# Score passes of 32 rows put into four row tiles of TensorE, in a hybrid MLA and forgetting-attention block

## The chip, the core and the metric

The kernel runs on one core of one Trainium2 chip. The metric is the device time of one execution in microseconds, lower being better. Three runs of the kernel before took 632.3, 632.51 and 634.76 us; their median is 632.51 us. A profile was taken of one further execution of the same program.

## What is computed

One decoder layer over 528 positions (16 learned meta tokens ahead of 512 real ones) of width 1024. A single projection of the normalised input gives the inputs of two attention branches and of their gates. Both branches have 16 heads of width 64 and a causal softmax. The branches differ in what is added to the product of query and key:

```python
q_m = concat([q_nope, rope(q_pe, pos)])          # 64 + 32 wide
k_m = concat([k_nope, broadcast(k_pe)])          # the 32-wide rotary key is one for all heads
o_mla = causal_block_attention(q_m, k_m, v_mla, MLA_SCALE)

cum = cumsum(log_sigmoid(f_logit + fox_forget_b))
o_fox = causal_block_attention(fq, fk, fv, FOX_SCALE, cum)    # logit[t,s] += cum[t] - cum[s]

y_mla = (o_mla * silu(z_mla)) @ w_br_mla
y_fox = (o_fox * silu(z_fox)) @ w_br_fox
mixed = (sigmoid(gate_a) * y_mla + sigmoid(gate_b) * y_fox) @ w_out
out = h + rmsnorm(mixed)                          # meta tokens dropped
```

In the softmax of a row the term `cum[t]` is the same for all keys, so the kernel adds only the keys' part, `-cum[s]`.

## The kernel before

**Precision.** Float32 products are made of TensorE passes over operands that were split into a high and a low part (`wh` and `wl` of a weight, `uTh` and `uTl` of the input, entries 0 and 1 of `hlq` and `hlk` for queries and keys). A product is high by high, low by high and high by low. The weights are split as they arrive: ScalarE copies the high part (line 116) and GpSimd subtracts it for the low one (line 92). Their loads are issued on SyncE's queue (line 107) into three buffers (`wraw`).

**Stages.** The attention part goes over 8 pairs of heads, and for each pair first the forgetting branch (FoX, `br` is 1), then MLA (`br` is 0): 16 stages (line 681). A stage of TensorE is, in this order: scores of query blocks 0, 1 and 2 (`scores(0)`), the value products of the stage before (`values`, tile `ov`), scores of block 3 (`scores(1)`), and then filling work in steps: the projections for the next stage (`fq`, `fk`, `v`, `mq`, `mk`), the silu gates (`z`), the transposes of the values (`vt`, `vm`), between which the normalisations `norm(0)` and `norm(1)` are emitted (lines 725 to 737). TensorE keeps this written order (`manual_schedule`, line 415). The other engines and SyncE's queue are ordered by the framework's scheduler, which may move an instruction ahead of others that are not ready.

**Scores.** The two heads of a pair lie in partitions 0 to 63 and 64 to 127 (`hs`), so that each matmul fills 64 of the 128 rows of the array, and the two heads' matmuls are issued one behind the other. `sets` (lines 584 to 590) lists the passes over a piece of keys: the three passes of the split 64-wide product and then

- for FoX one pass with `ONE` as the stationary and `CT` as the moving operand: two rows of ones per head against two rows of `-cum/scale`, high and low part, the other 62 rows zero;
- for MLA two passes with `QP`, which holds 32 rows of the high part of the rotated query and 32 rows of its low part per head: one against `KPH`, which holds the high part of the rotary key twice, and one against `KPL`, which holds the low part of the key in the upper 32 rows of each head and zeros in the lower 32.

So FoX has 4 passes per piece and MLA has 5. Query block b sees 144 + 128 b keys. The pieces (`banks`, lines 600 and 601) are 144 and 272 columns for blocks 0 and 1, side by side in one PSUM bank per head; 400 columns for block 2 in another bank per head; and for block 3 columns 0 to 271 and 272 to 527 in two banks per head. The pool `stp` has four banks in all. VectorE reads a bank, adds the mask and finds the row's extreme (line 620, `nb`), ScalarE makes the exponentials (line 628), `norm` divides and splits the probabilities into `pn` (lines 655 and 656, the meta columns on GpSimd, lines 642 to 647), and eight DMA transposes a stage (line 661) bring them into `pt` for the value products, six for blocks 0 to 2 and two for block 3.

**Other transfers on SyncE's queue.** `CT` is loaded from `c_dram` by two transfers a pair (line 242; for pair 0 by four straight from `ch`, line 395), `QP` from `qpe_dram` by one transfer a pair (line 462). After the attention, the branch products (`py`), the gates (`pg`) and the output product (`po`) follow; the change does not touch them.

Of the kernel before, what the change touches and what calls it, by code (L numbers as in the profile page):

```python
# [11 lines left out]
F32 = mybir.dt.float32  # L12
F32R = mybir.dt.float32r
# [10 lines left out]
S = 512  # L24
# [25 lines left out]
def f32(ap):  # L50
    return ap.bitcast(F32)
# [3 lines left out]
def block_kernel(ctx: ExitStack, tc: tile.TileContext, x, meta_tokens, pre_norm_g, w_in, fox_forget_b,  # L55
                 mla_q_norm_g, mla_kv_norm_g, w_uq, w_ukv, w_br_mla, w_br_fox, w_out, post_norm_g,
                 rope_tok, rope_pe, out):
    nc = tc.nc
# [26 lines left out]
    def mm(*a, **k):  # L85
        nc.tensor.matmul(*a, **k)  # L86
# [4 lines left out]
    def split_lo(eng, lo, src, hi):  # L91
        eng.tensor_tensor(out=lo, in0=src, in1=f32(hi), op=ALU.subtract)  # L92
# [118 lines left out]
    ONE = fx.tile([128, 128], F32R, tag="ONE", name="ONE")  # L211
    nc.gpsimd.memset(f32(CT), 0.0)
    nc.gpsimd.memset(f32(ONE), 0.0)
    for h in range(2):
        nc.gpsimd.memset(f32(ONE[64 * h : 64 * h + 2, :]), 1.0)
    hls = {}

    def hl_done(key, n, w):
# [16 lines left out]
    def k_fox(pr):  # L235
        halves = hl_done(("k", 1, pr), L, HALF)

        def done(i, ps):
            halves(i, ps)
            if pr and i:  # L240
                for h in range(2):
                    nc.sync.dma_start(f32(CT[64 * h : 64 * h + 2, :]), c_dram[:, 2 * pr + h, :])
        return unit(f"fk{pr}", win_w(O_FK, pr), u_act, KD, ALLT, done)


# [2 lines left out]
    with ExitStack() as ph:  # L248
# [141 lines left out]
        nc.vector.scalar_tensor_tensor(out=ch[:, 1], in0=fa[:, 0], scalar=-1.0 / SC_FOX, in1=f32(ch[:, 0]),  # L390
                                       op0=ALU.mult, op1=ALU.subtract)

        for i in range(2):
            for h in range(2):
                nc.sync.dma_start(f32(CT[64 * h + i : 64 * h + i + 1, :]), f32(ch[h : h + 1, i]))
        for i in range(2):
            nc.sync.dma_start(c_dram[i], f32(ch[:, i]))
        run(qk[7:])
# [14 lines left out]
    with ExitStack() as att:  # L413
# [4 lines left out]
        stp = att.enter_context(tc.tile_pool(name="stp", bufs=4, space=PSUM))  # L418
        ovp = att.enter_context(tc.tile_pool(name="ovp", bufs=1, space=PSUM))

        QP = ac.tile([128, S], F32R, tag="QP", name="QP")
        KP = [ac.tile([128, L], F32R, tag=n, name=n) for n in ("KPH", "KPL")]
        maskt = ac.tile([128, L + 16], BF16, tag="maskt", name="maskt")
        nc.gpsimd.memset(maskt, 0.0)
# [12 lines left out]
            nc.gpsimd.memset(pn[b // 3][:, :, PN_STEP * b % 15, :], 0.0)  # L437
        for r in range(4):
            nc.vector.tensor_copy(KP[0][32 * r : 32 * r + 32], kpT)
        nc.gpsimd.memset(f32(KP[1]), 0.0)  # L440
        for h in range(2):
            split_lo(nc.vector, KP[1][64 * h : 64 * h + 32], kpT, KP[0][0:32])
        lctx.close()
        gpool = gctx.enter_context(tc.tile_pool(name="gpool", bufs=1, side="right"))
        gT = [gpool.tile([128, KD, S], F32, tag=n, name=n) for n in ("gT0", "gT1")]
# [3 lines left out]
        def q_mla(pr):  # L449
            kv = wukv.rearrange("p (h a e) -> p a h e", a=2, e=HD)  # L450

            def wrap(w):
                mw[pr] = w
                return (lambda k: w[k][0]), (lambda k: w[k][1])
            get = weights(lambda: [wuqh[:, k, 2 * pr : 2 * pr + 2, 0:NOPE] for k in range(2)]
                          + [kv[:, i, 2 * pr : 2 * pr + 2, :] for i in range(2)], wrap)

            halves = hl_done(("q", 0, pr), S, S)

            def q_done(i, ps):  # L460
                halves(i, ps)
                nc.sync.dma_start(f32(QP), qpe_dram[2 * pr : 2 * pr + 2].rearrange("h i x f s -> (h i x f) s"))
            return unit(f"mq{pr}", get, cq_act, 2, REAL, q_done)


# [111 lines left out]
        def attention(br, pr):  # L577
# [3 lines left out]
            nm_ = f"{br}{pr}"  # L581
            q, k = hls["q", br, pr], hls["k", br, pr]

            def sets(h, b, c0, w):
                hs = slice(64 * h, 64 * h + 64)
                qs, ks = slice(128 * b, 128 * b + 128), slice(c0, c0 + w)
                out = [(q[hs, i, qs], k[hs, j, ks]) for i, j in ((0, 0), (1, 0), (0, 1))]
                if br:
                    return out + [(ONE[hs], CT[hs, ks])]
                return out + [(QP[hs, qs], KP[i][hs, ks]) for i in range(2)]  # L590

            sums, sfs = {}, {}

# [4 lines left out]
            def scores(g):  # L598

                banks = (((0, 0, 144, 0), (1, 0, 272, 144)), ((2, 0, 400, 0),)) if g == 0 else \  # L600
                    (((3, 0, HALF, 0),), ((3, HALF, L - HALF, 0),))

                def fn():
                    if g == 0:
                        for t in ("nb", "su", "ri"):
                            sums[t] = aw.tile([128, 2, 4], F32, tag=t, name=f"{t}{nm_}")
                    sfs[g] = aw.tile([128, 2, (2 * SF_STEP + 400, L)[g]], F32, tag=f"sf{g}", name=f"sf{nm_}{g}", bufs=1)
                    for ib, parts in enumerate(banks):
                        ps = [stp.tile([128, 512], F32, tag="st", name=f"st{nm_}{g}{ib}{h}") for h in range(2)]
                        for b, c0, w, o in parts:  # L610
                            for i, ops in enumerate(zip(*(sets(h, b, c0, w) for h in range(2)))):
                                for h, (Q, K) in enumerate(ops):
                                    mm(ps[h][:, o : o + w], Q, K, start=(i == 0), stop=(i == 4 - br))
# [270 lines left out]
```

## Time and profile before

| | |
|---|---|
| median of the runs | 632.51 us (632.3 to 634.76) |
| span of the profiled execution, first to last instruction | 630.9 us |
| mean granted TensorE clock | 0.996 |
| TensorE matmul busy | 608.6 us, 96% |
| VectorE, ScalarE, GpSimd busy | 315.0, 342.9, 263.3 us |
| matmuls | 3890 |
| score matmuls (tile `st`): split product, `ONE` by `CT`, `QP` by `KPH`, `QP` by `KPL` | 480, 80, 80, 80 |
| scores and values, first to last | 71.9 us to 426.1 us |
| DMA transposes `pt` | 128, median 2.5 us from issue to landing |

The profile's times are of one execution, which has its span in the trace; the three runs have only their times. The span lies 1.6 us under the median of the runs. Matmuls overlap: one of 272 columns is shown as 0.29 us long, but the next on the same rows can start 0.13 us after it. So the price of a matmul is read from the distance of the starts and not from the lengths. In a timeline, like instructions that follow each other are one row with their count; the first column is the start in microseconds from the start of the span and the second the length of the whole row.

### The profile page before, as it was taken

The numbers are of one execution on the slowest core, as the hardware profiler recorded it, in microseconds if no ns is written. First come the engines' busy times: TensorE is split into PE (matmuls) and PEld (weight loads), VectorE is DVE, ScalarE is ACT, GpSimd is POOL, SyncE is SP. The second block draws the span as 40 slices with busy tenths as digits, with TensorE's granted clock in tenths as the row PEclk, the third lists the DMA queues.
The fourth block names the chain that finished last, engine by engine and source line by source line (L and its number), as shares of the span: only waits on it lengthen the run. The fifth ranks groups of instructions, "written<-read, shape, count | busy, mean of one in ns | idle before, by whom it ended". The sixth has DMA issues, their size and how long they took to land.

```text
span 630.9 us, 11084 instructions
## 1 busy us (share of the span) xinstructions
PE 608.6 (96%) x3890; PEld 515.7 (82%) x3890; DVE 315.0 (50%) x883; ACT 342.9 (54%) x774; POOL 263.3 (42%) x266
## 2 busy tenths in 40 slices
PE   3999989999999999999999999999999999999996
PEld 2879767988988889889889888878888888888885
DVE  3757557467476565674673765648222022113134
ACT  5656478378477575774784776757322232232321
POOL 3224633734344353343343443542544444444620
PEclk9999989999999999999999999999999999999999
DMA  8442657856656577467467665761532333333702
GB/s 284 123 84 54 138 147 188 205 143 153 168 135 137 145 148 163 113 162 174 101 157 175 116 153 149 158 166 38 162 93 80 97 99 100 101 100 113 255 34 100
DMA packets 204864, 85.38 MB, mean 135 GB/s; under 512 B 122684, under 2 KB 197820, under 8 KB 204808
## 3 DMA queue, kind: packets, MB, share of 16 engines
q1 hardware_dynamic: 204808, 84.67, 53.0%
q8 instruction: 30, 0.49, 0.3%
q14 instruction: 26, 0.21, 0.1%
HBM read 55.21 MB, written 4.26 MB: 94 GB/s over the span
## 4 chain that ended last, share of the span: by engine, by line
PE 89%; ACT 3%; DMA 3%; DVE 1%; issue 1%; POOL 1%; SPq 1%; DVEq 0%; POOLq 0%; ACTq 0%
PE py L86 14%; PE pg L86 14%; PE z L86 12%; PE v L86 8%; PE fk L86 7%; PE st L86 7%; PE po L86 7%; PE fq L86 7%; PE ov L86 5%; PE psm L86 3%; DMA pt<-pn 2%; PE mq L86 2%; PE mk L86 1%; PE vt L89 1%; DMA wsr<-in_w_in_dram 1%
## 5 line engine op out<-in xcount | busy, mean ns | idle before, releaser
L92 POOL TENSOR_TENSOR wl<-wraw,wh 128x1024 fp32r<-128x1024 f32 (+1 forms) x90 | 207.4, 2307 | 241.4 <-ACT wh L116 232.4
L116 ACT CAST wh<-wraw 128x1024 fp32r<-128x1024 f32 (+1 forms) x90 | 89.8, 1000 | 178.8 <-issue 84.1
L628 ACT ACTIVATE sf<-sf,nb 128x144 f32<-128x144 f32 (+3 forms) x128 | 71.9, 565 | 4.1 <-DVE nb L620 4.1
L655 ACT ACTIVATE pn<-sf,ri 128x128 f16<-128x128 f32 (+3 forms) x128 | 61.5, 551 | 15.0 <-ACT sf L628 14.8
L656 DVE SCALAR_TENSOR_TENSOR pn<-sf,ri,pn 128x128 f16<-128x128 f32 (+3 forms) x128 | 65.7, 553 | 7.9 <-ACT pn L655 7.9
L767 DVE SCALAR_TENSOR_TENSOR tb<-th,py 128x512 f32<-128x512 f32 x16 | 11.0, 686 | 107.4 <-PE py L86 107.4
L86 PE MATMUL z<-uTh,wh 128*128 128x512 f32 x128 | 51.4, 401 | 0.0
L86 PE MATMUL z<-uTh,wl 128*128 128x512 f32 x128 | 50.6, 395 | 0.0
L86 PE MATMUL z<-uTl,wh 128*128 128x512 f32 x128 | 50.4, 394 | 0.0
L86 PE MATMUL pg<-uTh,wh 128*128 128x512 f32 x128 | 50.1, 392 | 0.0
L86 PE MATMUL pg<-uTl,wh 128*128 128x512 f32 x128 | 49.8, 389 | 0.0
L86 PE MATMUL pg<-uTh,wl 128*128 128x512 f32 x128 | 49.8, 389 | 0.0
L86 PE MATMUL py<-gh,wh 128*128 128x512 f32 x128 | 49.8, 389 | 0.0
L86 PE MATMUL py<-gl,wh 128*128 128x512 f32 x128 | 49.8, 389 | 0.0
L86 PE MATMUL py<-gh,wl 128*128 128x512 f32 x128 | 49.8, 389 | 0.0
L620 DVE CUSTOM_DVE_ANT_0 sf<-st,maskt 128x272 f32<-128x272 f32 (+2 forms) x128 | 48.5, 435 | 0.0
L86 PE MATMUL st<-hlk,hlq 64*128 64x272 f32 (+3 forms) x480 | 48.0, 307 | 0.4 <-DVE nb L620 0.2
L642 POOL TENSOR_TENSOR mt<-sf,ri 128x96 f32<-128x96 f32 (+1 forms) x32 | 9.5, 297 | 83.7 <-DVE ri L637 62.1
L86 PEld LDWEIGHTS st<-hlk,hlq 64*128 64x128 f32 x480 | 35.4, 185 | 6.7 <-ACT wh L116 2.5
L86 PE MATMUL fk<-uTl,wh 128*128 128x256 f32 (+1 forms) x128 | 36.6, 286 | 0.0
L86 PE MATMUL fk<-uTh,wh 128*128 128x256 f32 (+1 forms) x128 | 36.5, 285 | 0.0
L86 PE MATMUL v<-uTh,wh 128*128 128x256 f32 (+1 forms) x128 | 36.5, 285 | 0.0
(186 smaller groups left out, 1449.4 us busy)
## 6 DMA issues: line engine op xcount, KB each, us to landing
wraw<-in_w_in_dram SPq DMA_DIRECT2D x56, 512.0 KB, 3.9
wraw<-in_w_br_fox_dram SPq DMA_DIRECT2D x8, 512.0 KB, 3.6
wraw<-in_w_br_mla_dram SPq DMA_DIRECT2D x8, 512.0 KB
wraw<-in_w_out_dram SPq DMA_DIRECT2D x8, 512.0 KB, 4.5
qpe_dram<-gT SPq DMA_DIRECT2D x8, 256.0 KB
QP<-qpe_dram SPq DMA_DIRECT2D x8, 256.0 KB, 2.8
pt<-pn SPq DMA_TRANSPOSE x128, 2.5
xr<-in_x_dram SPq DMA_DIRECT2D x4, 512.0 KB
```

The lines of the kernel that those rows point to most:

```text
L86: nc.tensor.matmul(*a, **k)
L89: nc.tensor.transpose(*a)
L92: eng.tensor_tensor(out=lo, in0=src, in1=f32(hi), op=ALU.subtract)
L116: nc.scalar.copy(wh[:, :n], raw[:, :n])
L620: nc.vector.tensor_tensor_reduce(out=sf_of(h, b)[:, c0 : c0 + w], in0=ps[h][:, o : o + w], in1=maskt[:, m0 : m0 + w], scale=-scale, scalar ...
L628: nc.scalar.activation(sf, sf, AF.Exp, bias=sums["nb"][:, h, b : b + 1], scale=-1.0, accum_out=sums["su"][:, h, b : b + 1])
L642: nc.gpsimd.tensor_tensor(out=mt, in0=src, in1=ri.unsqueeze(3).broadcast_to([128, 2, nb_, META]), op=ALU.mult)
L655: nc.scalar.activation(hi, sf, AF.Copy, scale=rib)
L656: nc.vector.scalar_tensor_tensor(out=lo, in0=sf, scalar=rib, in1=hi, op0=ALU.mult, op1=ALU.subtract)
L767: nc.vector.scalar_tensor_tensor(out=tb[br], in0=ths[i, br], scalar=1.0, in1=py, op0=ALU.add, op1=ALU.mult)
```

## The change

The passes that need no more than 32 rows are taken out of the 64-row passes, and issued as matmuls of 32 rows, each at one of the four row offsets 0, 32, 64 and 96. These are the `ONE` by `CT` pass of FoX and the `QP` by `KPL` pass of MLA. Each head has its offset 64 h and in addition a "side": side 0 is rows 64 h to 64 h + 31, and side 1 the next 32 rows. Two query blocks (or the two halves of block 3) lie on the two sides, so that four matmuls on different rows, into four different banks, follow each other.

- In `scores(0)` the 32-row matmuls are the first: block 2 on side 0, block 1 on side 1, then block 0 on side 1, each for both heads: six matmuls. Then the remaining 64-row passes follow (three for FoX, four for MLA), first those of blocks 0 and 1, then those of block 2. All four banks are taken at the start.
- In `scores(1)` the 64-row passes of both pieces are first and the four 32-row matmuls last. VectorE's reading of both pieces comes behind them.
- The number of matmuls and of weight loads is as before.
- `CT` and `ONE` have their two rows at all four offsets. `CT` is loaded by four transfers a pair (eight for pair 0).
- `KPL` is filled at all four offsets, and a new tile `QU` holds the high part of the rotated query in the lower 32 rows of each head; two more transfers a pair load it behind `QP`.

```diff
-    for h in range(2):
-        nc.gpsimd.memset(f32(ONE[64 * h : 64 * h + 2, :]), 1.0)
+    for r in range(4):
+        nc.gpsimd.memset(f32(ONE[32 * r : 32 * r + 2, :]), 1.0)
...
-                for h in range(2):
-                    nc.sync.dma_start(f32(CT[64 * h : 64 * h + 2, :]), c_dram[:, 2 * pr + h, :])
+                for r in range(4):
+                    nc.sync.dma_start(f32(CT[32 * r : 32 * r + 2, :]), c_dram[:, 2 * pr + r // 2, :])
...
-        nc.gpsimd.memset(f32(KP[1]), 0.0)
-        for h in range(2):
-            split_lo(nc.vector, KP[1][64 * h : 64 * h + 32], kpT, KP[0][0:32])
+        for r in range(4):
+            split_lo(nc.vector, KP[1][32 * r : 32 * r + 32], kpT, KP[0][0:32])
...
                 nc.sync.dma_start(f32(QP), qpe_dram[2 * pr : 2 * pr + 2].rearrange("h i x f s -> (h i x f) s"))
+                for h in range(2):
+                    nc.sync.dma_start(f32(QU[64 * h + 32 : 64 * h + 64]),
+                                      qpe_dram[2 * pr + h, 0].rearrange("x f s -> (x f) s"))
...
-                if br:
-                    return out + [(ONE[hs], CT[hs, ks])]
-                return out + [(QP[hs, qs], KP[i][hs, ks]) for i in range(2)]
+                return out if br else out + [(QP[hs, qs], KP[0][hs, ks])]
+
+            def quarter(h, side, b, c0, w):
+
+                rs = slice(64 * h + 32 * side, 64 * h + 32 * side + 32)
+                qs, ks = slice(128 * b, 128 * b + 128), slice(c0, c0 + w)
+                return (ONE[rs], CT[rs, ks]) if br else ((QP, QU)[side][rs, qs], KP[1][rs, ks])
...
+                    def quarters():
+                        sides = [(1 - g ^ ib, ps, part, n == 0) for ib, ps in enumerate(pss)
+                                 for n, part in enumerate(banks[ib][::-1])]
+                        if g == 0:
+                            sides = [sides[2], sides[0], sides[1]]
+                        for side, ps, (b, c0, w, o), first in sides:
+                            for h in range(2):
+                                Q, K = quarter(h, side, b, c0, w)
+                                mm(ps[h][:, o : o + w], Q, K, start=(g == 0 and first), stop=(g == 1),
+                                   skip_group_check=not first)
...
+                    if g == 0:
+                        quarters()
+                    else:
+                        rows(0)
+                        rows(1)
+                        quarters()
+                    for ib, parts in enumerate(banks):
+                        ps = pss[ib]
+                        if g == 0:
+                            rows(ib)
```

`rows(ib)` is the loop of before over the pieces of one bank and the passes that `sets` still lists.

More of the change, by code (lines that the diff above doesn't have):

```diff
@@ L391, in block_kernel @@
                                        op0=ALU.mult, op1=ALU.subtract)
-        for i in range(2):
-            for h in range(2):
-                nc.sync.dma_start(f32(CT[64 * h + i : 64 * h + i + 1, :]), f32(ch[h : h + 1, i]))
+        for r in (0, 2, 1, 3):
+            for i in range(2):
+                nc.sync.dma_start(f32(CT[32 * r + i : 32 * r + i + 1, :]), f32(ch[r // 2 : r // 2 + 1, i]))
         for i in range(2):
@@ L419, in block_kernel @@
         ovp = att.enter_context(tc.tile_pool(name="ovp", bufs=1, space=PSUM))
-        QP = ac.tile([128, S], F32R, tag="QP", name="QP")
+        QP, QU = (ac.tile([128, S], F32R, tag=n, name=n) for n in ("QP", "QU"))
         KP = [ac.tile([128, L], F32R, tag=n, name=n) for n in ("KPH", "KPL")]
@@ L439, in block_kernel @@
             nc.vector.tensor_copy(KP[0][32 * r : 32 * r + 32], kpT)
-        nc.gpsimd.memset(f32(KP[1]), 0.0)
-        for h in range(2):
-            split_lo(nc.vector, KP[1][64 * h : 64 * h + 32], kpT, KP[0][0:32])
+        for r in range(4):
+            split_lo(nc.vector, KP[1][32 * r : 32 * r + 32], kpT, KP[0][0:32])
         lctx.close()
@@ L607, in fn, with rows @@
                     sfs[g] = aw.tile([128, 2, (2 * SF_STEP + 400, L)[g]], F32, tag=f"sf{g}", name=f"sf{nm_}{g}", bufs=1)
-                    for ib, parts in enumerate(banks):
-                        ps = [stp.tile([128, 512], F32, tag="st", name=f"st{nm_}{g}{ib}{h}") for h in range(2)]
-                        for b, c0, w, o in parts:
+                    pss = [[stp.tile([128, 512], F32, tag="st", name=f"st{nm_}{g}{ib}{h}") for h in range(2)]
+                           for ib in range(len(banks))]
+                    def quarters():
[8 more added lines that the diff above has]
+                                   skip_group_check=not first)
+                    def rows(ib):
+                        for b, c0, w, o in banks[ib]:
                             for i, ops in enumerate(zip(*(sets(h, b, c0, w) for h in range(2)))):
                                 for h, (Q, K) in enumerate(ops):
-                                    mm(ps[h][:, o : o + w], Q, K, start=(i == 0), stop=(i == 4 - br))
+                                    mm(pss[ib][h][:, o : o + w], Q, K, start=(g == 1 and i == 0),
+                                       stop=(g == 0 and i == 3 - br), skip_group_check=(b == 0))
+                    if g == 0:
[8 more added lines that the diff above has]
+                            rows(ib)
                         for b, c0, w, o in parts:
```

## The prediction

> **What bounds the kernel now.** I read the page first: the busy times, and the chain of work that ended last.
>
> ```profile
> span 630.9 us, 11084 instructions
> PE 608.6 (96%) x3890; PEld 515.7 (82%) x3890; DVE 315.0 (50%) x883; ACT 342.9 (54%) x774; POOL 263.3 (42%) x266
> ...
> PE 89%; ACT 3%; DMA 3%; DVE 1%; issue 1%; POOL 1%; SPq 1%; DVEq 0%; POOLq 0%; ACTq 0%
> ```
>
> TensorE carries 89% of the chain, so a TensorE nanosecond saved or added in the attention stages is one of the span. Next, the chain in order of time over one MLA stage (30 score matmuls, then 20) and the FoX stage behind it (24, then 16).
>
> ```profile
> 186.72 2.29 PE st L86 x30
> 189.01 1.97 PE ov L86 x26
> 190.98 1.42 PE st L86 x20
> ...
> 210.35 1.88 PE st L86 x24
> 212.23 1.97 PE ov L86 x26
> 214.20 1.17 PE st L86 x16
> ```
>
> The two kinds of stage differ by one pass, so one pass costs 2.29 - 1.88 = 0.41 us in the first scores and 1.42 - 1.17 = 0.25 in the second. Five passes are 2.05 and 1.25; the remaining 0.24 and 0.17 us are paid once per visit. The timeline of that MLA stage shows what a pass consists of.
>
> ```profile
> 186.65 0.56 PE L86 MATMUL st<-hlk,hlq 64*128 64x144 f32 x6
> 187.04 0.27 PE L86 MATMUL st<-KPH,QP 64*128 64x144 f32 x2
> 187.15 0.27 PE L86 MATMUL st<-KPL,QP 64*128 64x144 f32 x2
> 187.26 0.59 PE L86 MATMUL st<-hlk,hlq 64*128 64x272 f32 x6
> 187.69 0.29 PE L86 MATMUL st<-KPH,QP 64*128 64x272 f32 x2
> 187.82 0.29 PE L86 MATMUL st<-KPL,QP 64*128 64x272 f32 x2
> 187.94 0.71 PE L86 MATMUL st<-hlk,hlq 64*128 64x400 f32 x6
> 188.49 0.34 PE L86 MATMUL st<-KPH,QP 64*128 64x400 f32 x2
> 188.66 0.35 PE L86 MATMUL st<-KPL,QP 64*128 64x400 f32 x2
> 188.94 0.41 PE L86 MATMUL ov<-pt,vm 80*64 80x512 f16 x2
> ```
>
> From start to start, a pair (both heads at once) takes 0.11 us at 144 columns, 0.125 at 272 (187.69 to 187.94 for two) and 0.18 at 400 (187.94 to 188.66 for four). The sum, 0.415, is the pass again. 400 columns per 0.18 us is the streaming rate; 144 columns should then take 0.065, so a floor of 0.11 holds there: the next weights on the same rows.
>
> **What a change of row tiling costs.** Before has no matmul of 32 rows. It has changes between 128 and 64 rows, shown here by two rows of matmuls at the entry and the weight loads behind it:
>
> ```profile
> 186.10 0.39 PE L86 MATMUL z<-uTl,wh 128*128 128x512 f32 x1
> 186.33 0.39 PE L86 MATMUL z<-uTh,wl 128*128 128x512 f32 x1
> ```
>
> ```profile
> 186.75 0.19 PEld L86 LDWEIGHTS st<-hlk,hlq 64*128 64x128 f32 x2
> ```
>
> z matmuls start every 0.23 us, so the array was free for another at 186.56. The first 64-row weights began only at 186.65, 0.09 later; the second ones, which go in while the first pair streams, at 186.75. So streaming restarted 0.19 to 0.20 us late: a wait for the array to run empty, then a weight load that nothing covers. At the exit the value products start at 188.94 where 188.84 was due. The 0.24 and 0.17 per visit say the same. I take 0.20 per change. The Trainium skill (TensorEngine Tiling (Array Packing), Key Properties) says that changing the tiling mode, and not just the tile, drains TensorE. It speaks against this change and names no size; the row above agrees for 128 to 64, and no run here shows 64 to 32.
>
> **TensorE's part.** In the first scores the change adds a visit in 32-row tiling ahead of the 64-row passes. The entry from `z` or `v` is paid as before. Blocks 2 and 1 stream together, then block 0 behind block 1: the longer of 0.18 and 0.125 + 0.065, so 0.19 us in place of 0.41. Then comes one more change of tiling: 0.20. Net -0.02. In the second scores 272 and 256 columns stream together, 0.125 in place of 0.25, and the change from 64 to 32 rows costs 0.20: net +0.075. Per stage that is +0.055, for 16 stages **+0.9 us**. The bounds: with a free change (0), -0.345 a stage, -5.5 us in all; with four streams taking as long as two pairs in turn (only pairs are seen in before), +0.40 a stage, +6.4. I take 0.20, because every change in before pays about that. The Trainium skill (TensorE: Matmul & The Clock Gate, Part 3: Packing small matmuls) gives four row tiles the span of one matmul plus about 4 ns for each further tile, and no charge for entering; by that alone it would be the -5.5.
>
> **What sits on SyncE's queue.** The other cost is in the transfers. For FoX, two more `CT` loads per pair, and for MLA two `QU` loads. The FoX stage at 166.95:
>
> ```profile
> 174.05 1.18 SPq L661 DMA_TRANSPOSE pt<-pn  x1
> 175.32 0.39 SPq L242 DMA_DIRECT2D CT<-c_dram  x1
> 175.80 1.20 SPq L661 DMA_TRANSPOSE pt<-pn  x1
> 177.09 0.39 SPq L242 DMA_DIRECT2D CT<-c_dram  x1
> 177.57 8.18 SPq L661 DMA_TRANSPOSE pt<-pn  x6
> ```
>
> The eight transposes fill the queue (1.36 us each in the row of six), and a `CT` load between two of them moves all later ones by 0.4 to 0.5 us (174.05 to 175.80 is 1.75). The scheduler has put the loads there although the pair that needs them is 35 us away; I expect the new ones at the same place. The last of the six is issued at about 184.4 (177.57 + 8.18 - 1.36), and `ov` needs it at 188.94.
>
> ```profile
> DMA to landing us min/median/max: 2.3/2.5/4.5
> ```
>
> That is a median landing at 187.0, 2.0 us in hand. But not everywhere:
>
> ```profile
> 227.64 1.30 SPq L661 DMA_TRANSPOSE pt<-pn  x1
> ```
>
> ```profile
> 232.32 0.71 PE L86 MATMUL ov<-pt,vm 80*64 80x512 f16 x2
> 232.66 2.00 PE L86 MATMUL ov<-pt,vp 128*64 128x512 f16 x24
> ```
>
> ```profile
> 358.16 4.93 DMA pt<-pn
> ```
>
> Here the last transpose took almost 5 us, and the value products already waited (0.71 us for a row that takes 0.41; the chain itself goes through the transpose). In these two stages any delay counts in full. The delay is 2 x 0.45 = 0.9 for `CT`; up to 0.15 because blocks 0 and 1 are complete a little later (0.39 + 0.71 us for three passes against 0.95 for four); and some for `QU`, which holds up, in the MLA stage before, the weight load behind the transposes:
>
> ```profile
> 153.36 0.53 SPq L462 DMA_DIRECT2D QP<-qpe_dram  x1
> 153.99 8.03 SPq L661 DMA_TRANSPOSE pt<-pn  x6
> 162.10 0.54 SPq L107 DMA_DIRECT2D wraw<-in_w_in_dram  x1
> ```
>
> That load feeds a ScalarE copy that stands ahead of the FoX exponentials; of its 1 us I let 0 to 0.5 come through and take 0.15. So 0.9 + 0.15 + 0.15 = 1.2 us, twice: **+2.4 us**. In the other FoX stages it fits into the 2 us; in the MLA stage just shown the six are issued by 162.0 and land by 164.5 at the median, before the next stage even begins at 166.95, so nothing shows. Bounds: 0 (the scheduler puts the loads behind the transposes, or the late landings don't recur) to 5 (three or four stages wait over 1 us).
>
> The first stage is bound by the same queue:
>
> ```profile
> 86.15 0.35 SPq L462 DMA_DIRECT2D QP<-qpe_dram  x1
> 86.60 11.15 SPq L661 DMA_TRANSPOSE pt<-pn  x8
> ```
>
> ```profile
> 99.47 0.38 PE L86 MATMUL ov<-pt,vm 80*64 80x512 f16 x1 [1.04 <-DMA pt<-pn]
> ```
>
> `QU` behind `QP` puts two issues of about 0.5 us ahead of the eight, and TensorE waits at their end already: **+1.0 us** (0 to 1.5).
>
> Costed at nothing: four more `CT` loads at the start, about 0.6 us each, since the queue's next work that anything waits for is some 2 us off and the first FoX scores start at 71.9; the memsets and two more subtractions for `KPL`, far ahead of the first MLA scores at 96; all four banks taken at once, since VectorE has read them several us before; the later read of block 3, because VectorE reaches it after `norm(0)` work anyway. If any of that cover fails, it costs a microsecond once, or a tenth per stage.
>
> **Sum.** 0.9 + 2.4 + 1.0 = +4.3 us on the profiled 630.9, to 635.2. The profiled execution lies 1.6 us under the median, and I keep that: 632.5 + 4.3 = **636.8 us**. About 0.5% (3.2 us) is what a measurement of this kernel can tell from no change: 629.3 to 635.7.
>
> **Rivals.**
>
> *The change of tiling between 32 and 64 rows is free* (faster). Weight loads on other rows overlap with running matmuls already: the two heads' loads are one row of two above. If a smaller tile counts as only another place, TensorE gains 5.5 us, and 0 to 3.4 of it goes back to the waits for transposes: 627.0 to 630.4, say 628.7. It decides from a price under 0.17 us per change (0.345 / 2). Against it: every change in the trace between 64 and 128 rows pays, in both directions. Chance 0.13.
>
> *The queue's cover holds* (same). TensorE loses 0.9, and the added transfers cost 0 to 1.5: 633.4 to 634.9, say 634. For it: the queue's order is the scheduler's, and a shift may move the late landings into MLA stages. Chance 0.30.
>
> *Four streams share what two had* (slower by more). The 32-row pass takes as long as before, 0.41 and 0.25, and the change of tiling comes on top: +6.4 for TensorE, +2 for the waits: 641. Nothing in before shows four at once. Chance 0.10.
>
> My forecast, 635 to 639, has 0.47; it is the likeliest.
>
> **The numbers.** Slower by over 0.5%: most of the forecast and all of the third rival, 0.50. Same: the second rival, the lower end of the forecast and some of the first, 0.39. Faster: most of the first, 0.11. The range for 8 in 10 runs from 629.5, inside the first rival, to 642.0, above the third.
>
> **What would show it.** First scores in their kind of stage within 0.05 us of 2.29 and 1.88, second ones 0.05 to 0.1 longer than 1.42 and 1.17. A gap of 0.2 us between the last 32-row and the first 64-row matmul; four 32-row matmuls of different rows starting within a few hundredths. Four `CT` loads among the FoX transposes, the last issued 1 us later, and `ov` waiting in about two FoX stages more than now, and 1 us more in the first. I am wrong if no gap stands between the two tilings, if four streams start in pairs, or if the loads come behind the transposes.

## The result, and the profile after

The changed kernel takes 641.81 us in the median of five runs (641.21 to 642.51), the kernel before 632.3 us in the runs beside it: the ratio is 1.0145, with a 95% interval of 1.0125 to 1.0164. The change costs 9.5 us. The forecast was +4.3 (636.8 us); the direction is right and the value lies just inside the range (629.5 to 642.0), but outside the 635 to 639 of the forecast proper, and the size is off by more than a factor of two. The two profiled executions have spans of 630.9 and 640.2 us, +9.3. Of the 65 runs of the kernel before that were taken beside the experiments, those with a mean granted clock of 0.995 or more took 630.9 to 633.4 us and those below it 632.5 to 637.4, and all five of the changed kernel have 0.988 to 0.990.

The page of the changed kernel, its span, busy times and shares of the chain:

```profile
span 640.2 us, 11161 instructions
PE 612.3 (96%) x3890; PEld 513.7 (80%) x3890; DVE 319.6 (50%) x885; ACT 343.0 (54%) x774; POOL 263.0 (41%) x267
...
PE 88%; DVE 6%; DMA 2%; SPq 2%; ACT 2%; issue 1%; DVEq 0%; ACTq 0%
```

TensorE has as many matmuls as before. What is new is VectorE: 6% of the chain where it had 1%. The chain in order of time, over the FoX and the MLA stage that answer to those shown of before:

```profile
172.74 1.84 PE st L86 x22
...
176.55 1.24 PE st L86 x15
...
192.51 2.27 PE st L86 x28
194.78 1.97 PE ov L86 x26
196.75 1.60 PE st L86 x16
198.38 0.64 DVE gT L707
...
201.03 0.66 PE vt L89 x4
```

The first scores are 1.84 and 2.27 where they were 1.88 and 2.29. The second scores of FoX are 1.24 (1.17). Those of MLA end when `fq` starts; the row's 1.60 runs a little over that, and the timeline below gives 1.5 (1.42). Behind them, in the MLA stage alone, the chain leaves TensorE for VectorE and comes back at `vt`, the transposes of the values. TensorE's waits (us in total, times, longest) show the same place, and another one:

```profile
PE st L86 <- DMA QU<-qpe_dram: 4.6, 1, 4.6
PE vt L89 <- DVE nb L651: 3.0, 6, 0.5
PE st L86 <- DVE nb L651: 2.0, 2, 1.8
```

None of the three is among the waits of before at this size. The third lies in the first FoX scores and costs nothing: before, TensorE waited 1.33 and 1.58 us in `mk` a little later, and after it no longer does.

**How far the two kernels drift apart.** Three rows of the chain of each serve as marks: the second scores of the first MLA stage, the value products of the MLA stage in which before waited for its late transpose, and the last second scores. First before, then after:

```profile
101.48 1.41 PE st L86 x16
...
232.39 2.28 PE ov L86 x23
...
408.51 1.42 PE st L86 x20
```

```profile
106.40 1.49 PE st L86 x18
...
238.96 1.97 PE ov L86 x26
...
417.52 1.50 PE st L86 x18
```

At the first mark after is 4.92 us late (106.40 - 101.48), at the last 9.01 (417.52 - 408.51). So half of the loss is there when the second scores of the first MLA stage begin, and another 4.1 us come by those of the last one. The second mark reads 1.97 where before had 2.28: the landing that was late there is no longer late.

**TensorE itself.** The timeline of the MLA stage, first scores, then second:

```profile
192.44 0.45 PE L86 MATMUL st<-KPL,QP 32*128 32x400 f32 x2
...
192.45 0.46 PE L86 MATMUL st<-KPL,QU 32*128 32x272 f32 x4
...
192.84 0.56 PE L86 MATMUL st<-hlk,hlq 64*128 64x144 f32 x6
...
197.63 0.28 PE L86 MATMUL st<-KPH,QP 64*128 64x256 f32 x2
...
197.84 0.39 PE L86 MATMUL st<-KPL,QP 32*128 32x272 f32 x2
...
197.85 0.39 PE L86 MATMUL st<-KPL,QU 32*128 32x256 f32 x2
...
198.16 0.50 PE L86 MATMUL fq<-uTh,wh 128*128 128x512 f32 x1
```

Four matmuls of 32 rows start within 0.01 us of each other, and in the second scores `fq` follows 0.32 us behind them, which is one piece of 272 columns (0.125) and a change of tiling: they stream at once. The visit of six in the first scores takes 0.40 us to the first 64-row matmul (192.44 to 192.84), against 0.19 + 0.20 forecast. So a change between 32 and 64 rows costs what one between 64 and 128 does. Per stage, first and second scores together change by -0.02 + 0.08 in MLA and -0.04 + 0.07 in FoX.

**The wait in the MLA stages.** VectorE and `vt` in before, from the timeline, and then in after:

```profile
193.21 0.70 DVE L656 SCALAR_TENSOR_TENSOR pn<-sf,ri,pn 128x128 f16<-128x128 f32 x2
193.83 0.43 DVE L620 CUSTOM_DVE_ANT_0 sf<-st,maskt 128x272 f32<-128x272 f32 x1
...
194.51 0.60 PE L89 MATMUL vt<-ident,vT 128*128 128x128 f32 x4
```

```profile
199.01 1.60 DVE L687 SCALAR_TENSOR_TENSOR pn<-sf,ri,pn 128x128 f16<-128x128 f32 x4
200.53 0.43 DVE L651 CUSTOM_DVE_ANT_0 sf<-st,maskt 128x272 f32<-128x272 f32 x1
...
201.03 0.66 PE L89 MATMUL vt<-ident,vT 128*128 128x128 f32 x4 [0.53 <-DVE nb L651]
```

`vt` takes a bank of the pool `stp`, the one that held the first piece of block 3. Before, two subtractions (`pn`) stand ahead of the read of that piece, after four. The two more cost VectorE 0.90 us (1.60 - 0.70). By the timelines the second scores start at 190.91 before and at 196.68 after, so the read starts 2.92 us behind them before (193.83 - 190.91) and 3.85 after (200.53 - 196.68), and `vt` waits 0.53 us for the bank. From the start of the second scores to the start of the next FoX scores, after is 0.80 us longer in six of the MLA stages, 0.08 of it in the scores.

**The first MLA stage.** SyncE's queue in after, and the chain behind it:

```profile
86.92 0.33 SPq L463 DMA_DIRECT2D QU<-qpe_dram  x1
...
87.77 0.35 SPq L461 DMA_DIRECT2D QP<-qpe_dram  x1
88.23 9.28 SPq L692 DMA_TRANSPOSE pt<-pn  x7
97.56 0.57 SPq L463 DMA_DIRECT2D QU<-qpe_dram  x1
...
98.56 1.28 SPq L692 DMA_TRANSPOSE pt<-pn  x1
```

```profile
99.73 4.07 PE st L86 x16
103.80 2.59 PE ov L86 x26
```

One `QU` load stands ahead of the transposes, the other behind seven of them. It lands 2 us after its issue at 97.56, and TensorE, which needs it for its first matmuls, stops for 4.62 us. What follows the stop is slow too: first scores of 4.07 us instead of 2.27, value products of 2.59 instead of 1.97. The granted clock goes with that (busy times of a window; the clock is the number behind the counts):

```profile
100.00:112.00 12.00, 12.00 (x94) 9.36 (x94) 7.73 (x31) 7.69 (x24) 1.25 (x4) 0.79 0.59 150
```

It is 0.79 where before has 1.00; in each microsecond from 100 to 105 it is 0.50. Before has a slow stretch too, earlier: 0.50 from 91 to 94 us, behind its two waits in `mk`. When the first MLA scores begin, the changed kernel is 1.07 us ahead (94.67 against 95.74). The 4.9 us are thus a balance: the stop is 3.6 us longer than the wait of 1.04 that before has in this stage, the slow rows add 1.8 and 0.6, and 1.1 had been gained. The Trainium skill (TensorE: Matmul & The Clock Gate, Part 1: The HAM clock gate) says that TensorE drops to half its clock after about 3.4 us without work and needs about as much work to come back. The 4.62 us and the rows of nearly double length agree; the slow stretch of before doesn't fit it, since its two waits, of 1.33 and 1.58 us with 0.6 us of work between them, are each far shorter.

### The profile page after: what moved, and what is told of

Read it like the earlier page. It is cut to its first block, busy times and chain, and to the rows that moved or that the text cites. A ratio compares the mean times of both kernels' runs of the same rounds, so it can differ in the third digit from the quotient of the medians.

```text
span 640.2 us, 11161 instructions
## 1 busy us (share of the span) xinstructions
PE 612.3 (96%) x3890; PEld 513.7 (80%) x3890; DVE 319.6 (50%) x885; ACT 343.0 (54%) x774; POOL 263.0 (41%) x267
## 4 chain that ended last, share of the span: by engine, by line
PE 88%; DVE 6%; DMA 2%; SPq 2%; ACT 2%; issue 1%; DVEq 0%; ACTq 0%
PE z L86 14%; PE py L86 14%; PE pg L86 13%; PE st L86 9%; PE v L86 7%; PE po L86 7%; PE fk L86 7%; PE ov L86 5%; PE fq L86 5%; PE psm L86 3%; PE mq L86 2%; PE vt L89 1%; PE mk L86 1%; DVE pn L687 1%; DMA wsr<-in_w_in_dram 1%
## 5 line engine op out<-in xcount | busy, mean ns | idle before, releaser
L86 PE MATMUL st<-hlk,hlq 64*128 64x272 f32 (+3 forms) x480 | 45.7, 314 | 2.1 <-DVE nb L651 2.0
```

## The experiments

The theory: two prices are paid, neither of them by TensorE's tiling. One is the order of block 3 (reads after both pieces), which costs six waits for a bank; the other is the queue of the first MLA stage. Its rivals are named at each run. Ratios are to the kernel before on the same chip (632.8 to 633.0 us). The edits are shown in part, against the changed kernel unless another is named.

### The order of block 3 alone

The kernel before with the order of the change, but all passes in 64 rows; no `QU`, `CT` loaded as before:

```diff
-                rs = slice(64 * h + 32 * side, 64 * h + 32 * side + 32)
+                rs = slice(64 * h, 64 * h + 64)
...
-                return (ONE[rs], CT[rs, ks]) if br else ((QP, QU)[side][rs, qs], KP[1][rs, ks])
+                return (ONE[rs], CT[rs, ks]) if br else (QP[rs, qs], KP[1][rs, ks])
```

> The kernel before with the changed order of the passes alone: the pass that the change puts into 32 rows is first in the first scores and last in the second, and both banks are read behind it, but it fills 64 rows as before, with no QU and the CT loads of before. Theory one: VectorE's order in the MLA stages becomes that of the changed kernel and the value transposes wait 0.7 us in each: 636 to 637.5. Theory two: no 32-row tiling, so the time of before, 632 to 633.

637.95 us, ratio 1.008 (1.0049 to 1.0111): +5.1 (+4.4 between the spans) with no 32-row matmul in the kernel, 0.45 above the stretch of theory one. The wait is the same one:

```profile
PE vt L89 <- DVE nb L649: 3.3, 6, 0.6
```

The first MLA stage loses nothing here. So the order alone is worth about half of the loss, and the other half must lie in what this kernel leaves out.

### The loads of QU earlier

The loads of `QP` and `QU` get a higher priority (the run qu_ahead), so that all three stand ahead of the transposes:

```diff
+                with tc.high_priority(offset=1000):
+                    nc.sync.dma_start(f32(QP), ...)
+                    for h in range(2):
+                        nc.sync.dma_start(f32(QU[64 * h + 32 : 64 * h + 64]), ...)
```

> The changed kernel, with the QP and QU loads given priority, so that all three stand ahead of the eight transposes of the first stage. Theory one (the 9.5 us are some 4.5 us once, because a QU load stood behind seven transposes in the first stage, some 0.7 us in each of seven MLA stages, because the value transposes wait for a PSUM bank that VectorE reads late, and under 1 us for the changes of row tiling): the 5 us stop of the first MLA scores and the slow clock behind it go, and about 2 us of waiting for transposes come in their place: 638 to 639.5. The wait of 0.7 us per MLA stage stays. Theory two (the 32-row tiling itself makes TensorE slower, and the rest is its consequence): also faster, since the first stage is the same for both.

642.24 us, ratio 1.0149 (1.0113 to 1.0185): no gain, the expectation was missed. The wait for `QU` is gone, but now the value products wait for the transposes, and they are as slow as the first scores were in the changed kernel (TensorE's timeline):

```profile
100.51 0.64 PE L86 MATMUL ov<-pt,vm 80*64 80x512 f16 x1 [2.90 <-DMA pt<-pn]
...
102.25 3.80 PE L86 MATMUL ov<-pt,vp 128*64 128x512 f16 x24
```

The last transpose is issued at 99.32. In before that is at about 96.4 (86.60 + 11.15 - 1.35), so with both `QU` loads ahead of the transposes, as the prediction had them, it comes 2.9 us later and not 1.0: the transposes begin 1.9 us later (88.51 for 86.60), and the rest is lost within their row, in which a `CT` load now stands. The price sits in the queue and not in the place of one load.

### A bank of its own for the value transposes

On top of the run just told, `vt` takes its bank from the pool of the value products and `vm` from the accumulators':

```diff
-                tp = stp.tile([128, 512], F32, tag="st", name=f"vt{br}{pr}")
+                tp = ovp.tile([128, 512], F32, tag="ov", name=f"vt{br}{pr}")
...
-                tp = stp.tile([128, 512], F32, tag="st", name=f"vm{br}{pr}")[:, 0:128]
+                tp = acc(f"vm{br}{pr}")[:, 0:128]
```

> The changed kernel with the loads ahead as in the run qu_ahead, and with the value transposes written to banks of other pools, so that they need none that the second scores hold. Theory one: the wait in the MLA stages goes, 4.5 to 5 us less than qu_ahead: 633.5 to 634.5; what is left over before is the changes of tiling (under 1 us) and the first stage. Theory two: the same as qu_ahead within 1 us.

649.99 us, ratio 1.0272 (1.0241 to 1.0303): missed by far. No `vt` waits for `nb` any more, and an MLA stage is only 0.1 us longer than in before, but the accumulators' pool is now short of a bank:

```profile
PE z L86 <- DVE sil L576: 13.7, 8, 3.0
```

So the wait for the bank could be removed, and that 0.7 us go with it; as a repair it is worthless, since another tile then waits longer.

### 32 rows in the first scores alone

Block 3 as in before (64-row passes, each piece read when it is complete), with a second tile of ones for it; loads as in the run qu_ahead (the run first_scores_only):

```diff
+                if b == 3:
+                    return out + ([(ON2[hs], CT[hs, ks])] if br else [(QP[hs, qs], KP[i][hs, ks]) for i in range(2)])
...
-                        quarters()
-                    else:
-                        rows(0)
-                        rows(1)
...
-                        if g == 0:
-                            rows(ib)
+                        rows(ib)
```

> The 32-row tiling in the first scores alone, loads ahead; the second scores (block 3) as before the change, with their 64-row passes and reads bank by bank. Theory one: VectorE's order in the MLA stages is again that of before, no wait for the bank; first scores 0.02 to 0.04 us shorter each: -0.5 us, and 1 to 2 us lost in the first stage: 632.5 to 634. Theory two: about half of the per-stage loss of the changed kernel stays: 635 to 636.

635.67 us, ratio 1.0037 (1.0016 to 1.0057), 1.7 above the stretch of theory one and inside that of theory two. The trace decides for the first: VectorE has its old order in the MLA stages and no `vt` waits. The drift is 4.9 us when the first FoX stage behind the first MLA stage begins, and 2.7 at the end: nothing is lost any more behind the first stage. What is left is the first stage, where its queue is that of the second run, with the granted clock at 0.72 from 100 to 112 us.

### The first pair's loads on another queue

For the first pair, `QP` and `QU` are loaded by GpSimd's queue, behind GpSimd's work on `pn`. This was put into three kernels: the changed one (the run h_after_gpsimd_queue), the one with 32 rows in the first scores alone (first_scores_gpsimd_queue), and the kernel before (where it is `QP` only).

```diff
-                nc.sync.dma_start(f32(QP), ...)
+                eng = nc.sync if pr else nc.gpsimd
+                if pr == 0:
+                    for t in (QP, QU):
+                        nc.gpsimd.tensor_copy(t[0:128, 0:16], pn[1][:, 1, 0, 32 : 48])
+                eng.dma_start(f32(QP), ...)
...
+                    eng.dma_start(f32(QU[64 * h + 32 : 64 * h + 64]), ...)
```

> The changed kernel with one thing different: for the first pair of heads the loads of QP and QU are issued by GpSimd, behind its work on pn, and no longer by SyncE ahead of the eight transposes (a copy of 16 columns from pn into QP and QU, overwritten by the loads, keeps them there in the order). Theory one (the first stage's price is SyncE's queue: it stands at the loads until the rotated queries have landed at about 86 us, while the first transposes could start at about 84.5): the +4.5 us of the first stage go, and a little more, since the queue of the kernel before stands there too; the waits of the value transposes for a bank, 0.6 to 0.7 us in each of seven MLA stages, stay. 636 to 637.5 us, span about 635. Rival (the first stage is bound by the landings of the loads themselves, on whatever queue): 640.5 to 642, with a wait of the first MLA scores for QP or QU of 3 us or more.

638.84 us (638.69 to 640.04), ratio 1.0084 (1.0055 to 1.0113); the expectation of 636 to 637.5 was 1.3 us too low, while the span of 635.9 is near the expected 635. The MLA waits are as before this edit, the stop of 4.62 us is gone, and two shorter ones of the value products remain in the first stage:

```profile
PE vt L89 <- DVE nb L655: 3.1, 6, 0.6
PE ov L86 <- DMA pt<-pn: 2.3, 2, 1.7
```

At the second scores of the first MLA stage this kernel is 0.5 us behind before (101.90 - 101.41), and the changed one 4.9. So the first stage's price is the queue's, and 4.4 us of it by the traces (4.92 - 0.49); the medians give 3.0 between the two kernels, or 3.6 when each is taken from the kernel before beside it (+9.5 and +5.9). What remains is again in the queue: all four `CT` loads of the next pair stand ahead of the transposes, which so begin at 86.50.

```profile
82.90 3.46 SPq L242 DMA_DIRECT2D CT<-c_dram  x4
```

> The run called first_scores_only (32-row passes in the first scores alone, block 3 as before the change), with the first pair's QP and QU loads on GpSimd's queue. Theory one: both prices are gone, the order of block 3 by its being as before, and the first stage's by the other queue. What is left is TensorE's gain in the first scores (0.03 to 0.06 us per stage, 0.5 to 0.9 us) and the two late landings that do not recur (0.8 us), and up to 1 us for the queue that also held up the kernel before: 630.0 to 632.0 us, span 628.5 to 630.5. Rival (the first stage keeps its price whatever queue issues the loads): 635 to 636.

632.1 us, ratio 0.9979 (0.9962 to 0.9996): at the top of the expectation, and the first version with 32-row passes that is not slower than before. Its span is 629.5, 1.4 under before; 0.5 of that is TensorE's gain in the first scores (8 x 0.04 + 8 x 0.02). The late landings, whose 0.8 us were expected to be gone, recur: the value products of four MLA stages take 2.08 to 2.51 us instead of 1.97, 1.0 us together. What makes up for them was not expected: in the seven later FoX stages `mk` is 0.1 to 0.2 us shorter, 1.2 us in all. In the stage shown below, the second half of `mk` starts in before as VectorE's subtraction for `hlq` ends; in this kernel, where VectorE's order in FoX stages has changed as well, that subtraction ends as `mk` begins. That the one causes the other was not tested. The chain of before and of this kernel:

```profile
225.71 0.91 PE mk L86 x6
```

```profile
225.15 0.72 PE mk L86 x6
```

> The kernel before with the first pair's QP load on GpSimd's queue and nothing else changed. The first stage of the kernel before waits 1.0 us for its last transpose, which is queued behind that load. Theory one (the queue is the bound of the first stage): 630.8 to 632.0, 0.5 to 1.5 us under the kernel before, and the wait of the value products in the first stage is gone. Rival (the transposes wait for the probabilities and not for the queue): 632.0 to 632.8, no change.

631.83 us, ratio 0.9968 (0.9951 to 0.9986): as expected. The transposes begin at 84.36 instead of 86.60, and the value products of the first stage no longer wait:

```profile
84.36 11.24 SPq L665 DMA_TRANSPOSE pt<-pn  x8
```

So the queue held up the kernel before as well, by about 1 us, and this one load gains as much without 32-row passes as the version above with them.

### Block 3's 32-row passes first

The changed kernel with the loads on GpSimd's queue, and in the second scores the 32-row passes ahead of the 64-row ones, so that the first piece is complete before the second:

```diff
-                    if g == 0:
-                        quarters()
-                    else:
-                        rows(0)
-                        rows(1)
-                        quarters()
+                    quarters()
                     for ib, parts in enumerate(banks):
                         ps = pss[ib]
-                        if g == 0:
-                            rows(ib)
+                        rows(ib)
```

> The changed kernel with the first pair's loads on GpSimd's queue, and in the scores of block 3 the 32-row passes first and the 64-row passes behind them, piece by piece, so that VectorE can read the first piece before the second is complete. By the order of VectorE's work in the built kernel, three normalisations now stand ahead of the two reads (four in the changed kernel, two before). Theory one (the bank of the value transposes comes late because the reads stand behind the normalisations): the wait of the value transposes falls from 0.6 to 0.7 us to 0.1 to 0.4 in each MLA stage; together with the first stage 632 to 635 us. Theory two (the wait comes from the 32-row matmuls holding all four banks at the end): no change of that wait, 636 to 637.5. A small loss is possible in both, since all four banks of block 3 must now be free at its start (block 2's are read last): at most 0.2 us per stage.

635.99 us, ratio 1.0042 (1.0022 to 1.0061), 1 us above the stretch of theory one and at the edge of theory two's. With three subtractions ahead of the reads, one `vt` still shows a wait of 0.2 us, where six waited up to 0.6. In the stage whose second scores start at 193.47 the first piece is complete at 194.71 and its read starts at 196.97, so the read waits for VectorE and not for the scores. But the edit has changed two things at once, VectorE's order and the place of the 32-row matmuls, so the two theories are parted only by the next run. The second scores of MLA are 1.65 us instead of 1.50.

### VectorE's order put back

The changed kernel with the loads on GpSimd's queue and TensorE's work as in the change. In MLA stages the subtractions of blocks 1 and 2 take their factor from a copy (`rj`) that a small added instruction makes after the reads of block 3:

```diff
+                    if g == 0 and br == 0:
+                        rj = aw.tile([128, 2, 3], F32, tag="rj", name=f"rj{nm_}", bufs=1)
+                        nc.vector.scalar_tensor_tensor(
+                            out=rj[:, :, 1:3], in0=sums["nb"][:, :, 3:4].broadcast_to([128, 2, 2]), scalar=0.0,
+                            in1=ri[:, :, 1:3], op0=ALU.mult, op1=ALU.add)
```

> The run h_after_gpsimd_queue (the changed kernel, block 3 in its new order, first pair's loads on GpSimd's queue; 638.8 us) with VectorE's order put back: in MLA stages the subtractions of blocks 1 and 2 take their factor from a copy that a small added VectorE instruction makes after the four reads of block 3, so that again two subtractions stand ahead of the reads and not four. TensorE's work is untouched. Theory one (the seven waits of the value transposes come from the order in which the scheduler laid VectorE's work, and not from the scores of block 3 being complete later: VectorE gets to the reads at about 3.1 us in the kernel before, and the scores are complete after 1.5): the waits of the value transposes for a bank go, and the 0.78 us per MLA stage with them: 633 to 634.5 us. Theory two (the banks come late because the scores are complete later, whatever VectorE's order): the waits stay, 638 to 640 us.

634.72 us, ratio 1.0022 (1.0001 to 1.0044), 0.2 above the expected stretch; 638.84 without the edit. The timeline shows why:

```profile
195.56 0.69 DVE L698 SCALAR_TENSOR_TENSOR pn<-sf,ri,pn 128x128 f16<-128x128 f32 x2
196.17 0.43 DVE L655 CUSTOM_DVE_ANT_0 sf<-st,maskt 128x272 f32<-128x272 f32 x1
...
196.91 0.60 PE L89 MATMUL vt<-ident,vT 128*128 128x128 f32 x4
```

The second scores begin at 193.24 here, so the first read starts 2.93 us behind them, as in before (2.92), although both pieces of block 3 are completed together at the end. No `vt` waits, and from the third stage to the last this kernel needs 4.2 us less than the one without the edit: six times 0.7. From the third stage to the last this kernel stays level with before (2.27 us behind at the start of that stretch, 2.15 at its end); those 2.2 us were lost in the first MLA stage, whose waits of 1.55 and 0.75 us came with a granted clock of 0.88 from 100 to 112 us.

### One more visit to the 32-row tiling

The kernel of 632.1 us, with the 32-row matmuls of block 0 issued behind the 64-row passes of block 1:

```diff
-                        quarters()
+                        quarters(0, 2)
...
-                        for b, c0, w, o in banks[ib]:
+                        for b, c0, w, o in banks[ib][::-1]:
+                            if b == 0:
+                                quarters(2, 3)
```

> The run first_scores_gpsimd_queue (632.1 us) with one more visit to the 32-row tiling in the first scores of every stage: the two 32-row matmuls of block 0 come behind the 64-row passes of block 1 and no longer behind the 32-row matmuls of blocks 2 and 1. The matmuls and their number are the same; added are two changes of tiling per stage. Theory one (a change between 32 and 64 rows costs about 0.2 us): the first scores take 0.4 to 0.5 us longer, 2.27 becomes 2.67 to 2.77 in MLA and 1.84 becomes 2.24 to 2.34 in FoX; 16 stages make 6.4 to 8 us, 638.5 to 640 us. Rival (a change between 32 and 64 rows is free): the first scores within 0.1 us of 2.27 and 1.84, 632 to 633.5 us.

637.17 us, ratio 1.0061 (1.0037 to 1.0086): +5.1 in the medians and +6.0 between the spans (635.5 and 629.5), below the expected +6.4, since the 1.0 us that four rows of value products waited without this edit are gone here. The price itself is as expected, in the chain and in the timeline:

```profile
188.25 2.72 PE st L86 x28
```

```profile
189.04 0.29 PE L86 MATMUL st<-KPH,QP 64*128 64x272 f32 x2
189.26 0.33 PE L86 MATMUL st<-KPL,QU 32*128 32x144 f32 x2
189.53 0.56 PE L86 MATMUL st<-hlk,hlq 64*128 64x144 f32 x6
```

First scores of MLA take 2.72 us instead of 2.27, those of FoX 2.29 instead of 1.84. Two changes of tiling were added, and 0.055 us of streaming (0.18 for blocks 2 and 1 and 0.065 for block 0 alone, in place of 0.19): (0.45 - 0.055) / 2 = 0.20 us per change. That settles the rival in which the change is free.

## Why the prediction was right in direction and wrong in size

The forecast by its terms, beside what the traces and runs show (shifts in the profiled executions):

| term of the sum | forecast | measured |
|---|---|---|
| TensorE's tiling, 16 stages | +0.9 | 8 x 0.06 + 8 x 0.03 = +0.7 |
| last transposes of two FoX stages | +2.4 | about -0.8 |
| the first MLA stage | +1.0 | +4.9 |
| the later read of block 3 | 0 | 6 x 0.72 = +4.3 |
| sum | +4.3 | +9.1 of 9.3 |

- **TensorE's tiling: right**, with its parts. The 0.20 us was taken from changes between 64 and 128 rows, and the added visit confirms it for 32 and 64. Four streams run at once, so the rival of 641 us, which lands nearest to the result, is wrong in its mechanism: its number was met by two other costs. That the result lies inside the range is therefore luck, since the range's upper end was set above that rival. The direction is luck in part too: the largest term of the forecast, +2.4, did not come, and what made the kernel slower is a term put at nothing and one put at 1.0 that measured 4.9. The Trainium skill (TensorEngine Tiling (Array Packing), Key Properties) says only that a change of mode drains the engine; the runs give the size, and it takes nearly all that the packing gains.
- **The step that failed first** is among those "costed at nothing": "the later read of block 3, because VectorE reaches it after `norm(0)` work anyway". With VectorE in the order of before the reason holds, as the run with that order put back shows: with 32-row passes last, the read still starts 2.93 us behind the start of the second scores, as in before (2.92). What was missed is that VectorE's order is laid by the scheduler at build time. In the changed kernel it put two more subtractions ahead of the reads, and the bank that `vt` needs came free 0.9 us later. The order of TensorE's passes alone brings this about, as the run without 32-row matmuls shows; that it is because the reads count as ready later is the likely reason, which no run tests. The cover named was `norm(0)`'s work ahead of the read; that work could grow, and who waits behind the read was not asked. The price named for a failure, a tenth per stage, was also too small: it is 0.7 in each MLA stage but the first and the last. FoX has no such wait: there one subtraction stands ahead of the first read, before and after.
- **The step mis-sized most** is the first stage. The forecast put both `QU` loads ahead of the eight transposes and counted two issues, +1.0 with 1.5 as the bound. In the trace one stands behind seven transposes. But the place isn't the cause: with all loads ahead the last transpose is issued 2.9 us later, and the loss is the same. The queue holds more than TensorE has slack for, whichever comes last stops TensorE for 3 to 5 us, and the clock falls behind the stop, which the forecast did not count: 1.8 + 0.6 us are rows at the low clock (4.07 for 2.27, 2.59 for 1.97). With the loads on another queue 4.4 of the 4.9 us are gone.
- **The late transposes did not come.** The two stages in which before waited are rid of their wait (1.97 instead of 2.28 in the first, 1.97 instead of 2.03 and a late start in the second), for -0.8 us together. In the FoX stage at 172.74 the last of the transposes is issued 4.5 us ahead of the value products:

```profile
181.14 0.66 SPq L242 DMA_DIRECT2D CT<-c_dram  x2
181.90 9.74 SPq L692 DMA_TRANSPOSE pt<-pn  x7
```

  (181.90 + 9.74 - 1.39 = 190.25; `ov` starts at 194.78.) That is 17.5 us behind the start of the stage's scores, as in before (184.4 - 166.95). Of the four `CT` loads only two stand among the transposes, as many as before; the others are ahead of the first one and behind the last, and a load behind the transposes is what the prediction named as a sign of being wrong. The sum also let the two late landings recur, with 0 as the bound if they don't, and they do not stay where they were. In the two kernels that have the loads of before in these stages most of the wait of 0.8 us is gone: 0.15 us is left in the run with the order of block 3 alone, 0.2 in the kernel before with one load on GpSimd's queue. What makes a landing late the runs do not show.

The version nearest to the change that isn't slower, 32 rows in the first scores alone with the first pair's loads on GpSimd's queue, is 0.9 us under before; moving the load alone gives 1.1. So row tiles of 32 are worth nothing here that these runs can measure.

## What to carry to other kernels

Where a change makes a result ready later, "its reader comes later anyway" isn't enough: ask what the scheduler will put in front of the reader, and who waits for the buffer behind it. Packing small passes pays only if the streaming saved is well above the changes of tiling around it, here 0.22 us saved against 0.20 paid per visit. And on a queue that is already the last thing to end in a stage, one more transfer is priced by the engine's whole stop, with its clock behind it, and not by the time of its issue.

## What the runs showed of the hardware

- Four matmuls on four row tiles of 32 start within 0.01 us of each other and stream at once; leaving or entering that tiling costs 0.20 us.
- Behind a stop of 4.62 us TensorE's granted clock was 0.50 for about 5 us (0.79 over 12 us). Shorter stops went with it sometimes: 1.33 and 1.58 us with 0.50 for 3 us in the kernel before, 1.55 and 0.75 us with 0.88 over 12 us in the run with VectorE's order put back, but 1.66 and 0.61 us with 1.00 in the same kernel without that edit. What decides the runs do not show.
